# Other SBUF addresses for the tiles that TensorE reads, and a reordered start, in a hybrid block kernel on one core

## The chip, the cores and the metric

The kernel runs on one core of one Trainium2 chip. The metric is the device time of one execution in microseconds (us). Three runs of the kernel before took 1031.94, 1033.36 and 1034.29 us; their median, 1033.36 us, is the time before. One further execution, 1032.51 us, was recorded by the hardware profiler: every row below is from it.

## The reference, cut to what matters

One layer of an encoder trunk on 1024 tokens by 1024 channels, all in float32:

```python
h = rms_norm(x, g_pre)
u = jnp.einsum('bsd,dn->bsn', h, w_in)          # 1024 -> 10*512 + 3*1024 columns
(pool_v, pool_g, conv_x, conv_gb, conv_gc, conv_g,
 sb_q, sb_k, sb_v, sb_g, merge) = jnp.split(u, ..., axis=-1)
y_pool = pool_mixer(pool_v, pool_w, pool_scale) * silu(pool_g)
y_conv = conv_mixer(conv_x, conv_gb, conv_gc, conv_w, conv_b) * silu(conv_g)
y_sb = stick_breaking_attention(sb_q, sb_k, sb_v) * silu(sb_g)
proj = einsum('bsnw,nwd->bsnd', stack([y_pool, y_conv, y_sb]), w_branch)
merged = sum over the branches of sigmoid(merge) * proj
out = x + rms_norm(merged @ w_out, g_post)
```

## The kernel before, in words

Every product runs on TensorE (PE) in a form of float32 that is split in two: a matrix is kept as a high part and a remainder (names ending in h, hi, or l, lo), and a product is three matmuls, high by high, high by remainder and remainder by high. ScalarE (ACT) writes the high part, and VectorE (DVE) or GpSimd (POOL) subtracts it from the raw matrix to get the remainder (`split`, L72 to L74). A matmul holds a 128x128 piece still and streams 512 columns of the other operand past it.

The work goes in stages.

- **Start (L258 to L311).** The eight row tiles of x (`xt`) are loaded, squared and summed on ACT (`junk`, L268), `rstd` comes from POOL (L272) and DVE scales the tile (L273). PE transposes each tile in eight pieces into the PSUM tile `xtp` (L283), ACT and DVE split that into `hh` and `hl` (L285, L286). Token half t=0 is made of tiles 0 to 3, half t=1 of tiles 4 to 7. Then come the first attention blocks K and Q (`half_block`, L183 to L191: 24 matmuls for each half of the tokens), whose results are split again into `khi`, `klo`, `qa` and `qb`.
- **Attention (L321 to L463)**, with the other Q, K, V and gate blocks laid between its parts. Its result is four `y_sb` tiles.
- **Projection of y_sb (L553 to L557).** `y_sb` is split into `yhi` and `ylo` in the pool `ysp`; 8 `branch_proj` calls (L482) of 2 x 12 matmuls each. Between them DVE builds `t1`, `t2`, `t3` and `t4` from the quarters of h (`build_quarters`, L508).
- **24 pairs (`run_pair`, L564).** Two blocks of `w_in` are multiplied with h at once in seven products instead of eight (the Strassen way). Each product (L530) is 12 matmuls; its streamed operand is a quarter of h (`hh`, `hl`; also `t4`, which is written over one of them) in four of the seven and `t1`, `t2` or `t3` in three. POOL makes the remainders of the seven weights.
- **Gated projections of the other two branches** lie between the pairs; their `yhi` and `ylo` are in the pool `ypp`. At the end the merged sums become the tiles `m` (L734), d = 0 to 3 in the pool `fin`, d = 4 to 7 in the pool `big`.
- **Out projection (`out_products`, L791)** with `m` held still and `oh`, `wo` streamed, then the post-norm.

The order of the instructions on each engine is made by the framework's scheduler. The addresses come from pools: a pool without a side is stacked on the left, from low addresses up, and one with `side="right"` is stacked from the top of the partition down. Where a tile starts follows from the sizes below it. In the kernel before, all tiles of left pools that PE reads start on a multiple of 64 bytes. The right side begins 32 bytes off such a multiple, and the tiles of right pools in the table all start 32 bytes off.

| tiles | read by | pool | bytes past a multiple of 64, before | after |
|---|---|---|---|---|
| `hh`, `hl`, `t4`, `oh`, `m` of d 4 to 7 | PE | `big` | 0 | 0 |
| `w_hi`, `w_lo`, `wo` | PE | `wsp`, `wo1` | 0 | 0 |
| `t1`, `t2`, `t3` (h and l) | PE | `quarters` | 32 | 0 |
| `yhi`, `ylo` of y_sb | PE | `ysp` | 32 | 0 |
| `yhi`, `ylo` of the other two branches | PE | `ypp` | 0 | 0 |
| `m` of d 0 to 3 | PE | `fin`, then `quarters` | 32 | 0 |
| `mr`, then `back` | ACT, DVE | `fin`, then `quarters` | 32 | 0 |
| `w_raw`, `s_raw`, `s`, `ysb`, tiles of `gates` | ACT, DVE, POOL | `wraw`, `sraw`, `ssum`, `ysb`, `gates` | 0 | 32 |
| `m1`, `u2`, `u3` | DVE | `tmps` | 32 | 32 |
| `proj`, `q` | DVE, a DMA | `stp` | 32 | 0 |

In the kernel before, 1056 matmuls stream an operand that starts 32 bytes off: 24 pairs x 3 products x 12 on `t1` to `t3`, and 16 x 12 on `y_sb`; 204 more hold such an `m` still.

Of the kernel before, what the change touches and what calls it, by code (L numbers as in the profile page):

```python
# [35 lines left out]
def hybrid_block_kernel(ctx, tc, x, g_pre, w_in, pool_w, pool_scale, conv_w, conv_b, w_branch, w_out, g_post, out):  # L36
# [221 lines left out]
    with tc.tile_pool(name="xp", bufs=1) as xp, tc.tile_pool(name="ps_s", bufs=2, space=PSUM) as ps_s:  # L258
        g_bc = xp.tile([P, D], F32, tag="g", name="g_bc")
        nc.scalar.dma_start(g_bc, g_pre.broadcast_to([P, D]))  # L260
        xns = []
# [28 lines left out]
        first_w = [next_w(0), next_w(0)]  # L290
        for i in range(4):
            transposed(i)
        for i in range(4, 8):
            normed(i)
        q_w = qkp.tile([P, 2, S], F32R, tag="vc", name="q_w", bufs=1)
        second_w = []
        for kh, ks in enumerate(HALVES):
            raw = wraw.tile([P, HALF], F32, tag="raw", name="w_raw")
            nc.sync.dma_start(raw, w_in[SB_Q, kh])
            split(raw, q_w[:, 0, ks], q_w[:, 1, ks], nc.gpsimd)  # L300
            second_w.append((q_w[:, 0, ks], q_w[:, 1, ks]))
        blocks = list(zip((first_w, second_w), (k_parts(0), q_parts(0))))
        for t in range(2):
            for ws, post in blocks:
                ps = ps_g.tile([P, HALF], F32, tag="g", name="g_ps")
                run(half_block(ps, ws, t))
                if t == 0 and post is blocks[0][1]:
                    for i in range(4, 8):
                        transposed(i)
                post(t, ps)  # L310
# [588 lines left out]
```

## Time and profile before

| | |
|---|---|
| median of three runs | 1033.36 us (1031.94 to 1034.29) |
| the profiled execution | 1032.51 us |
| its span, first to last instruction | 1030.7 us |
| PE busy | 997.1 us, 97% of the span, 4752 matmuls |
| DVE busy | 636.5 us, 62% |
| POOL busy | 453.0 us, 44% |
| ACT busy | 447.8 us, 43% |
| chain that ended last | PE 84%, ACT 5%, DVE 4%, POOL 3% |

A row of the timeline gives the start, the duration, the engine, the line of the kernel, the operation and its tiles, out<-in. A matmul's duration there (0.39 us and more for 512 columns) is longer than the distance to the next one, since matmuls are pipelined; how fast PE goes is read from the distance between starts. PEld is PE's load of the piece that is held still, which runs beside the matmuls.

### The profile page before, as it was taken

To read this page: it belongs to the slowest core of one execution; us is meant where nothing else is said; L and a number is where in the kernel's file an instruction comes from. 1 tells how busy PE (TensorE), PEld (TensorE's weight loads), DVE (VectorE), ACT (ScalarE), POOL (GpSimd) and SP (SyncE) were. 2 spreads that over 40 slices of the span, in tenths; PEclk is the share of its full clock that TensorE was granted. 3 is DMA by queue.
4 is the path that set the end of the run, shared out by engine and by line. 5 is a ranking of instruction groups with operands and counts; after the bars stand their busy time and mean duration, and the time that the engine had idled before them with its cause. 6 is when DMAs were issued, how large, how long until landed. Compare 5 with 4: busy or idle time off the path is not lost.

```text
span 1030.7 us, 13275 instructions
## 1 busy us (share of the span) xinstructions
PE 997.1 (97%) x4752; PEld 825.0 (80%) x4752; DVE 636.5 (62%) x847; ACT 447.8 (43%) x871; POOL 453.0 (44%) x359
## 2 busy tenths in 40 slices
PE   4999999999998999999999999999999999999997
PEld 3788888888887788888888888888888888887886
DVE  6556766767776968889686685566333434465133
ACT  6557668668664553332232233343332322354111
POOL 3134543634564015455445444445555565556000
PEclk9999999999999999999999999999999999999999
DMA  6101000100101442322212224455434533256033
GB/s 227 60 21 35 28 22 22 41 21 21 31 22 31 163 153 62 98 66 72 83 52 72 82 62 163 153 191 167 133 126 125 209 112 120 65 186 223 1 123 123
DMA packets 43986, 97.09 MB, mean 94 GB/s; under 512 B 5264, under 2 KB 5520, under 8 KB 43920
## 3 DMA queue, kind: packets, MB, share of 16 engines
q1 hardware_dynamic: 43776, 95.71, 28.5%
q8 instruction: 38, 0.62, 0.2%
q10 hardware_dynamic: 144, 0.52, 0.1%
q14 instruction: 28, 0.23, 0.1%
HBM read 73.15 MB, written 23.07 MB: 93 GB/s over the span
## 4 chain that ended last, share of the span: by engine, by line
PE 84%; ACT 5%; DVE 4%; POOL 3%; issue 2%; DMA 2%; SPq 0%; POOLq 0%; DVEq 0%; ACTq 0%
PE g_ps L539 26%; PE q_ps L539 17%; PE g_ps L189 12%; PE pp L491 11%; PE o_ps L796 8%; PE o L418 3%; PE tp L404 2%; DVE sn L386 2%; PE z L382 1%; PE z L379 1%; POOL w_lo L74 1%; POOL sp L388 1%; ACT sn L383 1%; DMA xt<-in_x_dram 1%; ACT sp L384 1%
## 5 line engine op out<-in xcount | busy, mean ns | idle before, releaser
L74 POOL TENSOR_TENSOR w_lo<-s,w_hi 128x512 fp32r<-128x512 f32 x95 | 132.4, 1394 | 181.6 <-ACT w_hi L73 179.1
L388 POOL TENSOR_TENSOR sp<-sp,sn 128x127 f32<-128x127 f32 (+3 forms) x64 | 81.2, 1272 | 132.9 <-DVE sn L386 69.0
L74 POOL TENSOR_TENSOR w_lo<-s_raw,w_hi 128x512 fp32r<-128x512 f32 x70 | 94.2, 1346 | 96.5 <-ACT w_hi L73 92.3
L386 DVE TENSOR_TENSOR_SCAN sn<-sn,zeros 128x128 f32<-128x128 f32 (+3 forms) x64 | 100.5, 1574 | 48.3 <-ACT sn L383 45.5
L73 ACT CAST w_hi<-s 128x512 fp32r<-128x512 f32 x96 | 59.6, 621 | 136.0 <-PE g_ps L539 65.7
L73 ACT CAST w_hi<-s_raw 128x512 fp32r<-128x512 f32 x70 | 43.4, 620 | 132.5 <-PE g_ps L539 52.6
L189 PE MATMUL g_ps<-hh,w_hi 128*128 128x512 f32 x240 | 99.4, 414 | 0.3 <-ACT hh L285 0.3
L189 PE MATMUL g_ps<-hl,w_hi 128*128 128x512 f32 x240 | 94.5, 394 | 0.3 <-DVE hl L286 0.3
L189 PE MATMUL g_ps<-hh,w_lo 128*128 128x512 f32 x240 | 94.5, 394 | 0.0
L539 PE MATMUL g_ps<-hh,w_hi 128*128 128x512 f32 x236 | 92.6, 392 | 0.0
L539 PE MATMUL g_ps<-hh,w_lo 128*128 128x512 f32 x236 | 92.1, 390 | 0.0
L539 PE MATMUL g_ps<-hl,w_hi 128*128 128x512 f32 x236 | 91.8, 389 | 0.0
L74 POOL TENSOR_TENSOR w_lo<-w_raw,w_hi 128x512 fp32r<-128x512 f32 x44 | 67.6, 1535 | 53.1 <-ACT w_hi L73 53.1
L491 PE MATMUL pp<-yhi,w_lo 128*128 128x512 f32 x192 | 75.0, 392 | 0.7 <-DVE g L717 0.7
L491 PE MATMUL pp<-ylo,w_hi 128*128 128x512 f32 x192 | 75.0, 392 | 0.0
L491 PE MATMUL pp<-yhi,w_hi 128*128 128x512 f32 x192 | 74.9, 391 | 0.0
L383 ACT ACTIVATE sn<-z 128x384 f32<-128x384 f32 (+2 forms) x96 | 47.9, 499 | 29.7 <-PE z L382 20.4
L232 DVE TENSOR_TENSOR wl<-tp,wh 128x512 fp32r<-128x512 f32 (+2 forms) x96 | 50.4, 544 | 15.4 <-ACT wh L405 14.9
L539 PE MATMUL q_ps<-hh,w_hi 128*128 128x512 f32 x148 | 58.0, 392 | 0.0
L539 PE MATMUL q_ps<-hh,w_lo 128*128 128x512 f32 x148 | 57.9, 391 | 0.0
L539 PE MATMUL q_ps<-hl,w_hi 128*128 128x512 f32 x148 | 57.5, 389 | 0.0
L133 DVE TENSOR_TENSOR s<-s_raw 128x512 f32<-128x512 f32 x48 | 41.9, 873 | 23.4 <-POOL w_lo L74 22.8
(205 smaller groups left out, 2423.8 us busy)
## 6 DMA issues: line engine op xcount, KB each, us to landing
s_raw<-in_w_in_dram SPq DMA_DIRECT2D x96, 256.0 KB, 2.6
pr<-proj SPq DMA_DIRECT2D x48, 256.0 KB, 3.5
proj<-g SPq DMA_DIRECT2D x20, 512.0 KB, 3.0
w_raw<-in_w_in_dram SPq DMA_DIRECT2D x34, 256.0 KB, 2.6
w_raw<-in_w_branch_dram SPq DMA_DIRECT2D x24, 256.0 KB, 2.6
xt<-in_x_dram SPq DMA_DIRECT2D x8, 512.0 KB, 7.9
proj<-proj SPq DMA_DIRECT2D x8, 512.0 KB, 2.7
wo_raw<-in_w_out_dram SPq DMA_DIRECT2D x16, 256.0 KB, 3.3
```

Of the source, the lines that this page charges most:

```text
L73: nc.scalar.copy(hi, raw)
L74: eng.tensor_tensor(out=lo, in0=raw, in1=f32(hi), op=ALU.subtract)
L133: nc.vector.tensor_tensor(out=o, in0=a, in1=b, op=how)
L189: nc.tensor.matmul(ps, l[:, a], r[k // 4][t][:, k % 4, :], start=(n == 0), stop=(n == 3 * KB - 1))
L232: nc.vector.tensor_tensor(out=o, in0=a, in1=f32(b), op=ALU.subtract)
L383: nc.scalar.activation(sn[:, c0:c1], z[:, :w], AF.Sigmoid, scale=-0.125)
L386: nc.vector.tensor_tensor_scan(out=rev, data0=rev, data1=zeros.to_broadcast([P, n]), initial=1.0, op0=ALU.mult, op1=ALU.max)
L388: nc.gpsimd.tensor_tensor(out=sp[:, 0:n - 1], in0=sp[:, 0:n - 1], in1=sn[:, 1:n], op=ALU.mult)
L418: nc.tensor.matmul(o[:, cs], vc[:, j, s, :], wt[j // 4][:, j % 4, cs], start=(j == 0 and wt is wl), stop=(j == i and wt is wh))
L491: nc.tensor.matmul(pp, l[:, a], r[:, HALVES[t]], start=(n == 0), stop=(n == 3 * NB - 1))
L539: nc.tensor.matmul(bank, l[:, a], r[:, j, :], start=(n == 0), stop=(n == 11))
L796: nc.tensor.matmul(ps, l[:, a], r[:, es], start=(d == 0 and n == 0), stop=(d == KB - 1 and n == 2))
```

## The change

Two things are changed.

**Addresses.** The pools `quarters`, `stp` and `ysp` move from the right side to the left. `wraw`, `ysb`, `sraw`, `ssum` and `gates` move from the left to the right, and `tmps` stays there under a later place. The tiles `m` of d 0 to 3, the two buffers for what comes back from DRAM (`mr`, now the two halves of `back`), `gpost_sb` and the last `junk` no longer have a pool of their own at the end: they take tiles of `quarters`. `wt` is opened ahead of `au`. The table above shows where the tiles come to lie.

**Start.** The mask is made first, in a tile of its own. `g_bc` is loaded through SP's queue as the third transfer instead of through ACT's beside the first, and the loads of the Q weights go ahead of x tiles 6 and 7. The remainders of the first two weights are made on POOL instead of DVE. The half-blocks K and Q of t=0 are each made in two parts of 256 columns, the first part from x tiles 0 and 1 alone: 96 matmuls of 256 columns take the place of 48 of 512. PE has 4800 matmuls in place of 4752.

```diff
-    wraw = op("wraw", 3)
+    wraw = op("wraw", 3, side="right")
@@ stationary()
-            yield loaded(src, nc.vector if n < 4 else nc.gpsimd)
+            yield loaded(src, nc.vector if 2 <= n < 4 else nc.gpsimd)
@@ half_block(ps, ws, t, cols=slice(0, HALF))
-                nc.tensor.matmul(ps, l[:, a], r[k // 4][t][:, k % 4, :], start=(n == 0), stop=(n == 3 * KB - 1))
+                nc.tensor.matmul(ps[:, cols], l[:, a], r[k // 4][t][:, k % 4, cols], start=(n == 0), stop=(n == 3 * KB - 1))
@@ start
-    ysb_pool = ysb_stack.enter_context(tc.tile_pool(name="ysb", bufs=4))
+    ysb_pool = ysb_stack.enter_context(tc.tile_pool(name="ysb", bufs=4, side="right"))
-        nc.scalar.dma_start(g_bc, g_pre.broadcast_to([P, D]))
+        load(0)
+        load(1)
+        nc.sync.dma_start(g_bc, g_pre.broadcast_to([P, D]))
+        load(2)
+        masks(xp.tile([P, P], F32, tag="future", name="future"))
+        normed(0)
+        normed(1)
+        first_w = [next_w(0), next_w(0)]
+        load(3)
+        load(4)
+        load(5)
+        transposed(0)
+        normed(2)
+        q_w = qkp.tile([P, 2, S], F32R, tag="vc", name="q_w", bufs=1)
+        second_w = list(q_weights())
+        transposed(1)
+        normed(3)
+        k_ps, q_ps = [ps_g.tile([P, HALF], F32, tag="g", name="g_ps") for _ in range(2)]
+        run(half_block(k_ps, first_w, 0, slice(0, 256)))
+        transposed(2)
+        run(half_block(q_ps, second_w, 0, slice(0, 256)))
+        transposed(3)
+        for i in range(4, 8):
+            if i > 5:
+                load(i)
+            normed(i)
+        for i, (ps, ws, post) in enumerate(((k_ps, first_w, k_post), (q_ps, second_w, q_post))):
+            for n in half_block(ps, ws, 0, slice(256, HALF)):
+                if i == 1 and n % 2 == 1:
+                    transposed(4 + n // 2)
+            post(0, ps)
@@ pools
-    tpool, close_t = pool_of("quarters", 6, side="right")
+    tpool = op("quarters", 6, reuse_waits="tile")
-    stp, close_stp = pool_of("stp", 2, side="right")
-    ysp, close_ysp = pool_of("ysp", 4, side="right")
+    ysp, close_ysp = pool_of("ysp", 4)
+    stp, close_stp = pool_of("stp", 2)
-    held["raw"] = op("sraw", 5, reuse_waits="tile")
-    held["sum"] = op("ssum", 3, reuse_waits="tile")
+    held["raw"] = op("sraw", 5, side="right", reuse_waits="tile")
+    held["sum"] = op("ssum", 3, side="right", reuse_waits="tile")
+    gpool = op("gates", 4, side="right", reuse_waits="tile")
@@ take_merged, taken_back
-            o = (held["m"].tile([P, 2, S], F32R, tag="m", name="m", bufs=4) if d < 4
-                 else bigp.tile([P, 2, S], F32R, tag="big", name="m"))
+            o = tpool.tile([P, 2, S], F32R, tag="t", name="m") if d < 4 else bigp.tile([P, 2, S], F32R, tag="big", name="m")
+        back = tpool.tile([P, 2, S], F32, tag="t", name="back")
-                m = held["m"].tile([P, S], F32, tag="mr", name="mr", bufs=2)
+                m = back[:, d % 2, :]
```

From the first matmul of the V block on, PE's instructions stand in the same order as before. The start is where the order changes, on PE, DVE and POOL.

PE before, from the end of K's half-block of t=0 on (`g_ps_268` is K, `g_ps_361` is Q, both 512 columns wide; `xt_219` and `xt_229` are x tiles 4 and 5, `xt_239` is tile 6):

```order
L189 MATMUL g_ps_268<-hh1_0_72,w_hi_159 128x512
L189 MATMUL g_ps_268<-hl1_0_76,w_hi_159 128x512
L189 MATMUL g_ps_268<-hh1_0_72,w_lo_160 128x512
L283 MATMUL xtp_293<-ident_82,xt_219 128x128 x4
L283 MATMUL xtp_300<-ident_82,xt_219 128x128 x4
L283 MATMUL xtp_307<-ident_82,xt_229 128x128 x4
L283 MATMUL xtp_314<-ident_82,xt_229 128x128 x4
L189 MATMUL g_ps_361<-hh0_0_70,q_w_259 128x512
L189 MATMUL g_ps_361<-hl0_0_74,q_w_259 128x512
L189 MATMUL g_ps_361<-hh0_0_70,q_w_259 128x512
L283 MATMUL xtp_321<-ident_82,xt_239 128x128 x4
L189 MATMUL g_ps_361<-hh0_0_70,q_w_259 128x512
```

PE after, from the end of Q's first 256 columns on (`g_ps_212` is K, `g_ps_213` is Q; `xt_153` is x tile 3, `xt_155` is tile 4):

```order
L190 MATMUL g_ps_213<-hl1_0_76,q_w_181 128x256
L190 MATMUL g_ps_213<-hh1_0_72,q_w_181 128x256 x2
L190 MATMUL g_ps_213<-hl1_0_76,q_w_181 128x256
L190 MATMUL g_ps_213<-hh1_0_72,q_w_181 128x256
L286 MATMUL xtp_276<-ident_82,xt_153 128x128 x4
L286 MATMUL xtp_283<-ident_82,xt_153 128x128 x4
L286 MATMUL xtp_368<-ident_82,xt_155 128x128 x2
L190 MATMUL g_ps_212<-hh0_0_70,w_hi_143 128x256
L190 MATMUL g_ps_213<-hh0_0_70,q_w_181 128x256
L286 MATMUL xtp_368<-ident_82,xt_155 128x128 x2
L286 MATMUL xtp_375<-ident_82,xt_155 128x128 x4
L190 MATMUL g_ps_212<-hl0_0_74,w_hi_143 128x256
```

Before, tiles 4 to 7 are transposed after K's whole half-block. Now tile 3 is transposed only after the first quarters of K and of Q, and the second quarters, which need tiles 2 and 3, come behind it.

DVE before, from the last remainders of tiles 2 and 3 on (`xtp_205` and `xtp_212` are tile 3):

```order
L286 TENSOR_TENSOR hl1_0_76<-xtp_198,hh1_0_72 128x4x128
L286 TENSOR_TENSOR hl0_0_74<-xtp_205,hh0_0_70 128x4x128
L286 TENSOR_TENSOR hl1_0_76<-xtp_212,hh1_0_72 128x4x128
L273 SCALAR_TENSOR_TENSOR xt_219<-xt_219,rstd_226,g_bc_109 128x1024
L273 SCALAR_TENSOR_TENSOR xt_229<-xt_229,rstd_236,g_bc_109 128x1024
L273 SCALAR_TENSOR_TENSOR xt_239<-xt_239,rstd_246,g_bc_109 128x1024
L270 TENSOR_SCALAR var_254<-ssq_252 128x1
L273 SCALAR_TENSOR_TENSOR xt_249<-xt_249,rstd_256,g_bc_109 128x1024
L74 TENSOR_TENSOR w_lo_510<-w_raw_507,w_hi_509 128x512
L232 TENSOR_TENSOR klo_350<-g_ps_268,khi_349 64x512
L286 TENSOR_TENSOR hl0_1_75<-xtp_293,hh0_1_71 128x4x128
```

DVE after, from the last remainder of tile 2 on (`xtp_276` and `xtp_283` are tile 3, `xt_155`, `xt_157`, `xt_306` and `xt_316` are tiles 4 to 7):

```order
L289 TENSOR_TENSOR hl1_0_76<-xtp_245,hh1_0_72 128x4x128
L274 TENSOR_SCALAR var_293<-ssq_291 128x1
L277 SCALAR_TENSOR_TENSOR xt_155<-xt_155,rstd_295,g_bc_109 128x1024
L274 TENSOR_SCALAR var_301<-ssq_299 128x1
L277 SCALAR_TENSOR_TENSOR xt_157<-xt_157,rstd_303,g_bc_109 128x1024
L274 TENSOR_SCALAR var_311<-ssq_309 128x1
L274 TENSOR_SCALAR var_321<-ssq_319 128x1
L277 SCALAR_TENSOR_TENSOR xt_306<-xt_306,rstd_313,g_bc_109 128x1024
L277 SCALAR_TENSOR_TENSOR xt_316<-xt_316,rstd_323,g_bc_109 128x1024
L289 TENSOR_TENSOR hl0_0_74<-xtp_276,hh0_0_70 128x4x128
L289 TENSOR_TENSOR hl1_0_76<-xtp_283,hh1_0_72 128x4x128
L289 TENSOR_TENSOR hl0_1_75<-xtp_368,hh0_1_71 128x4x128
```

Before, the remainders `hl` of tile 3 stand ahead of the scaling of tiles 4 to 7; now they stand behind all four.

POOL before, from the first `rstd` to the first remainder of a V weight:

```order
L272 TENSOR_TENSOR rstd_118<-var_116,expo_78 128x1
L272 TENSOR_TENSOR rstd_128<-var_126,expo_78 128x1
L272 TENSOR_TENSOR rstd_138<-var_136,expo_78 128x1
L272 TENSOR_TENSOR rstd_148<-var_146,expo_78 128x1
L272 TENSOR_TENSOR rstd_226<-var_224,expo_78 128x1
L272 TENSOR_TENSOR rstd_236<-var_234,expo_78 128x1
L272 TENSOR_TENSOR rstd_246<-var_244,expo_78 128x1
L171 AFFINE_SELECT future_458<-future_458 128x128
L74 TENSOR_TENSOR q_w_259<-w_raw_260,q_w_259 128x512
L74 TENSOR_TENSOR q_w_259<-w_raw_264,q_w_259 128x512
L272 TENSOR_TENSOR rstd_256<-var_254,expo_78 128x1
L74 TENSOR_TENSOR w_lo_522<-w_raw_519,w_hi_521 128x512
```

POOL after, over the same stretch:

```order
L276 TENSOR_TENSOR rstd_130<-var_128,expo_78 128x1
L276 TENSOR_TENSOR rstd_138<-var_136,expo_78 128x1
L74 TENSOR_TENSOR w_lo_144<-w_raw_141,w_hi_143 128x512
L276 TENSOR_TENSOR rstd_178<-var_176,expo_78 128x1
L74 TENSOR_TENSOR w_lo_150<-w_raw_147,w_hi_149 128x512
L276 TENSOR_TENSOR rstd_209<-var_207,expo_78 128x1
L74 TENSOR_TENSOR q_w_181<-w_raw_182,q_w_181 128x512
L74 TENSOR_TENSOR q_w_181<-w_raw_186,q_w_181 128x512
L276 TENSOR_TENSOR rstd_295<-var_293,expo_78 128x1
L276 TENSOR_TENSOR rstd_303<-var_301,expo_78 128x1
L276 TENSOR_TENSOR rstd_313<-var_311,expo_78 128x1
L276 TENSOR_TENSOR rstd_323<-var_321,expo_78 128x1
```

The `rstd` of tiles 2 and 3 now stand behind a remainder of a first weight each, and those of tiles 4 to 7 all stand behind the two remainders of the Q weights; before, only the last did.

## Rows read from the trace of the kernel before

**Rows 1.** The page, busy time of PE: us (share of the span) x instructions

```profile
PE 997.1 (97%) x4752; PEld 825.0 (80%) x4752; DVE 636.5 (62%) x847; ACT 447.8 (43%) x871; POOL 453.0 (44%) x359
```

**Rows 2.** Waits of PE in the whole span: us in total, times, longest

```profile
PE xtp L283 <- DVE xt L273: 10.2, 1, 10.2
PE xtp L283 <- DVE hl L286: 5.3, 2, 3.2
PE pp L491 <- DVE g L717: 0.7, 1, 0.7
```

**Rows 3.** Timeline of PE, first matmul of each product: start, duration

```profile
579.01 0.40 PE L539 MATMUL g_ps<-t2h,w_hi 128*128 128x512 f32 x1
...
581.82 0.40 PE L539 MATMUL g_ps<-hh,w_hi 128*128 128x512 f32 x1
...
584.57 0.40 PE L539 MATMUL q_ps<-t3h,w_hi 128*128 128x512 f32 x1
...
590.18 0.40 PE L539 MATMUL g_ps<-hh,w_hi 128*128 128x512 f32 x1
...
592.93 0.39 PE L539 MATMUL g_ps<-hh,w_hi 128*128 128x512 f32 x1
...
595.65 0.39 PE L539 MATMUL g_ps<-hh,w_hi 128*128 128x512 f32 x1
...
598.37 0.40 PE L539 MATMUL q_ps<-t2h,w_hi 128*128 128x512 f32 x1
```

**Rows 4.** Timeline of PE, every twelfth matmul, `ysp` (343) and `ypp` (744)

```profile
343.44 0.39 PE L491 MATMUL pp<-yhi,w_lo 128*128 128x512 f32 x1
...
346.24 0.39 PE L491 MATMUL pp<-yhi,w_lo 128*128 128x512 f32 x1
...
744.09 0.39 PE L491 MATMUL pp<-yhi,w_lo 128*128 128x512 f32 x1
...
746.81 0.39 PE L491 MATMUL pp<-yhi,w_lo 128*128 128x512 f32 x1
```

**Rows 5.** Stretches: us, PE, PEld, DVE, ACT, POOL busy (x), clock, DMA share, GB/s

```profile
378.00:690.00 312.00, 312.00 (x1355) 253.77 (x1354) 224.81 (x283) 99.67 (x164) 152.97 (x110) 1.00 0.30 95
908.00:926.00 18.00, 18.00 (x81) 14.90 (x80) 13.57 (x15) 10.36 (x16) 11.29 (x7) 1.00 0.73 246
340.00:376.00 36.00, 36.00 (x156) 28.89 (x155) 34.82 (x57) 19.84 (x35) 0.00 (x0) 1.00 0.51 175
956.00:1012.00 56.00, 56.00 (x245) 45.67 (x244) 14.64 (x30) 6.88 (x20) 2.74 (x5) 1.00 0.25 82
```

**Rows 6.** Timeline of the start, all engines, [idle before <-releaser]

```profile
7.61 1.06 ACT L268 ACTIVATE junk<-xt 128x1024 f32<-128x1024 f32 x1 [0.50 <-DMA xt<-in_x_dram]
...
16.82 3.27 PEld L283 LDWEIGHTS xtp<-ident,xt 128*128 128x128 f32 x16 [3.41 <-DVE hl L286]
...
21.92 5.75 DVE L273 SCALAR_TENSOR_TENSOR xt<-xt,rstd,g_bc 128x1024 f32<-128x1024 f32 x3
...
22.70 3.88 POOL L74 TENSOR_TENSOR q_w<-w_raw,q_w 128x512 fp32r<-128x512 f32 x2 [1.37 <-ACT q_w L73]
...
26.62 1.89 PEld L283 LDWEIGHTS xtp<-ident,xt 128*128 128x128 f32 x16
...
28.46 1.28 DVE L273 SCALAR_TENSOR_TENSOR xt<-xt,rstd,g_bc 128x1024 f32<-128x1024 f32 x1 [0.73 <-POOL rstd L272]
...
49.17 0.39 PE L189 MATMUL g_ps<-hh,w_hi 128*128 128x512 f32 x1
```

**Rows 7.** Groups by line and form: x count | busy, mean ns | idle before

```profile
L74 POOL TENSOR_TENSOR w_lo<-s_raw,w_hi 128x512 fp32r<-128x512 f32 x70 | 94.2, 1346 | 96.5 <-ACT w_hi L73 92.3 <-DVE pb L663 2.8 <-DVE s L133 1.3
...
L241 ACT CAST khi<-g_ps 64x512 fp32r<-64x512 f32 x16 | 9.3, 581 | 2.7 <-PE g_ps L189 2.6
...
L568 ACT COPY m<-g_ps 128x512 f32<-128x512 f32 x15 | 8.7, 580 | 0.0
...
L74 DVE TENSOR_TENSOR w_lo<-w_raw,w_hi 128x512 fp32r<-128x512 f32 x12 | 8.2, 687 | 1.1 <-ACT w_hi L73 0.9
```

More of the change, by code (lines that the diff above doesn't have):

```diff
@@ L164, in hybrid_block_kernel, with masks @@
     cnt = const.tile([P, PAD], F32, name="cnt")
-    def load_small():
+    def masks(future):
         nc.vector.memset(zeros, 0.0)
         nc.scalar.copy(ident_r, ident)
-        future = wraw.tile([P, HALF], F32, tag="raw", name="future")[:, 0:P]
         nc.vector.memset(future, 0.0)
@@ L173, in load_small @@
         nc.scalar.copy(mask_r, future)
+    def load_small():
         nc.sync.dma_start(pscale_sb, pool_scale)
@@ L259, in hybrid_block_kernel, with load, normed @@
         g_bc = xp.tile([P, D], F32, tag="g", name="g_bc")
-        nc.scalar.dma_start(g_bc, g_pre.broadcast_to([P, D]))
         xns = []
-        def normed(i):
+        def load(i):
             xt = xp.tile([P, D], F32, tag="xt", name="xt", bufs=8)
             nc.sync.dma_start(xt, x[i * P:(i + 1) * P, :])
+            xns.append(xt)
+        def normed(i):
+            xt = xns[i]
             junk = xp.tile([P, D], F32, tag="junk", name="junk")
@@ L286, in transposed @@
                 nc.vector.tensor_tensor(out=lo, in0=tp, in1=f32(hi), op=ALU.subtract)
-        for i in range(4):
-            normed(i)
[L290 to L310, printed above, removed]
+        def q_weights():
+            for kh, ks in enumerate(HALVES):
+                raw = wraw.tile([P, HALF], F32, tag="raw", name="w_raw")
+                nc.sync.dma_start(raw, w_in[SB_Q, kh])
+                split(raw, q_w[:, 0, ks], q_w[:, 1, ks], nc.gpsimd)
+                yield q_w[:, 0, ks], q_w[:, 1, ks]
@@ L311, in hybrid_block_kernel @@
+        for ws, post in ((first_w, k_post), (second_w, q_post)):
+            ps = ps_g.tile([P, HALF], F32, tag="g", name="g_ps")
+            run(half_block(ps, ws, 1))
+            post(1, ps)
     load_small()
@@ L319, in silu_block @@
         return block(post)
-    with tc.tile_pool(name="au", bufs=3) as au, \
-            tc.tile_pool(name="wt", bufs=3) as wtp, tc.tile_pool(name="ps_z", bufs=2, space=PSUM) as ps_z, \
+    with tc.tile_pool(name="wt", bufs=3) as wtp, \
+            tc.tile_pool(name="au", bufs=3) as au, tc.tile_pool(name="ps_z", bufs=2, space=PSUM) as ps_z, \
             tc.tile_pool(name="ps_w", bufs=2, space=PSUM) as ps_w, \
@@ L556, in hybrid_block_kernel @@
             build_quarters(d // 2)
+    close_stp()
     close_ysp()
-    close_stp()
-    tmps, close_tmps = pool_of("tmps", 1, side="right")
+    gpool = op("gates", 4, side="right", reuse_waits="tile")
+    tmps = op("tmps", 1, side="right", reuse_waits="tile")
     held["q"] = op("ps_q", 2, space=PSUM, reuse_waits="tile")
@@ L675, in pool_branch @@
         return last
-    gpool = op("gates", 4, reuse_waits="tile")
     def gate_pair():
@@ L774, in hybrid_block_kernel @@
     gs = gate_pair() + gate_pair()
-    close_tmps()
-    close_t()
-    held["m"] = op("fin", 1, side="right", reuse_waits="tile")
     next(coming_back)
@@ L785, in hybrid_block_kernel @@
     wo1p = op("wo1", KB, reuse_waits="tile")
-    fin = held["m"]
-    gpost_sb = fin.tile([P, D], F32, tag="gpost", name="gpost_sb")
+    fin = op("fin", 1, reuse_waits="tile")
+    late = tpool.tile([P, 2, S], F32, tag="t", name="late")
+    gpost_sb, junk = late[:, 0, :], late[:, 1, 0:HALF]
     nc.sync.dma_start(gpost_sb, g_post.broadcast_to([P, D]))
```

5 lines of the change are left out of this document (2 added, 3 removed).

## The prediction

> **What bounds the kernel now.** I read the page first. PE is busy 997.1 us of the 1030.7 us span [rows 1], so a term counts here if it makes PE's own work shorter or takes away a wait of PE. Next I read PE's waits: three concern this change, 10.2 us before the first transpose, 5.3 us in two pieces at later transposes, and 0.7 us near the end [rows 2]. The other waits lie in the attention stage, where nothing that PE reads changes its offset. Last I read the distance between matmul starts, because a busy PE is not a PE at its fastest. Seven products of a pair are shown, 12 equal matmuls each, with no wait between them [rows 3]. The two that stream `hh` late in the pair take 592.93 to 595.65 and 595.65 to 598.37, 2.72 us each, which is 226.7 ns for a matmul. The product on `t2` takes 2.81 us (579.01 to 581.82). `t3` and `t1` together take 5.61 us (584.57 to 590.18). An `hh` product that comes directly behind a run on `t` takes 2.75 us (581.82 to 584.57, and 590.18 to 592.93). The same kinds of weights, banks and shapes stand on both sides; what differs is the tile that is streamed.
>
> Two things could be behind that: the role of the tile (its place in the pair, what else reads it), or its address. Rows 4 separate them. `yhi` and `ylo` appear twice in the kernel, in code of one shape. In the pool `ysp`, 32 bytes off a multiple of 64, twelve matmuls take 2.80 us (343.44 to 346.24). In the pool `ypp`, on a multiple, they take 2.72 us (744.09 to 746.81) [rows 4]. So I take the offset of 32 bytes as the cause: 0.08 us for a product.
>
> A rule speaks against it. The Trainium skill ("SBUF — State Buffer", section "Operand start alignment") says that an operand need only start on a multiple of its element size, 4 bytes for fp32, and adds that this is about legality and that its runs timed nothing; by an engine that takes any such address alike, the address part would be worth 0. The trace differs: 2.80 us against 2.72 us.
>
> **The address part.** One whole pair takes 579.01 to 598.37, 19.36 us. Seven clean products would take 7 x 2.72 = 19.04 us. The pair loses 0.32 us, and 24 pairs lose 7.7 us. As a check, the stretch from 378 to 690 us is PE alone, with 1355 matmuls in 312.00 us; a clean stretch of 18.00 us counts 81, where 18.00/0.2267 = 79.4, so a window counts 1.6 too many at its edges [rows 5]. Then 312.00 - 1353.4 x 0.2267 = 5.2 us are lost there, and 312/19.36 = 16.1 pairs at 0.32 us are also 5.2 us.
>
> The projection of y_sb has 16 products on `ysp`, 0.08 us each: 1.3 us. In the out projection half of the `m` tiles are off; there the moved operand is the one held still. Its stretch from 956 to 1012 us counts 245 matmuls [rows 5], so 56.00 - 243.4 x 0.2267 = 0.8 us are lost; over its 384 matmuls (8 token tiles x 2 halves x 24) that is 1.3 us.
>
> After the change all of these tiles start on a multiple of 64. The sum is 7.7 + 1.3 + 1.3 = 10.3 us. A lower bound: the `hh` products behind a `t` product may keep their 0.03 us, since their own tile was never off (0.03 x 2 x 24 = 1.4 us), so 8.9 us. An upper bound is the sum itself, since it goes down to the clean pitch everywhere.
>
> **What goes off in exchange.** `w_raw`, `s_raw`, `s`, `ysb` and the tiles of `gates` now start 32 bytes off; ACT, DVE, POOL and DMAs read or write them. For ACT, writing a tile off a multiple takes 580 ns (`m1`, `m<-g_ps`) and on one 581 ns (`khi`) [rows 7]. So I cost ACT and DVE at 0. POOL touches no such tile before, and its price is unknown: the nearest row is its 1346 ns on aligned `s_raw` [rows 7]. Seven of those are 9.4 us in a pair of 19.36 us, so that a slower POOL stays hidden up to twice that time; I take 0, and the far end is a rival below.
>
> One cover gets thinner. From 340 to 376 us DVE is busy 34.82 of 36.00 us [rows 5]. There PE becomes about 1 us faster, and DVE must finish `t1` to `t3` for the first pair, so between 0 and all of the 1.3 us of that stage may come back as a wait. I keep it in the range.
>
> The 0.7 us wait at the end is one of `g`, behind the loads of `mr` [rows 2]. `back` sits in tiles of `quarters`, which come free earlier than the old end pool. I take 0.4 us saved, between 0 and 0.7.
>
> **The start.** What counts is when the V block begins, since from there on the order is unchanged: 49.17 us before [rows 6].
>
> - Gain at the front. Before, the first scaling waits until the second x tile is squared, at 7.61 to 8.67 us [rows 6]; `g_bc` shares the DMA queues with the first two tiles. Behind them it no longer does, so both tiles come about one 512 KB piece earlier, some 1.3 us (squares start at 7.61 us, and the row says the wait was for the DMA). PE starts about 1.3 us earlier.
> - The two remainders on POOL instead of DVE free 2 x 0.69 us of DVE and cost POOL 1.35 us or more each [rows 7], or 1.94 us beside a busy DVE (3.88 for two) [rows 6]. Behind them stand the `rstd` of tiles 2 and 3. That uses up the 1.3 us: tile 3 is scaled no earlier than before. The Trainium skill ("GPSIMD Engine Reference", section "4.1 Engine selection") advises VectorE for elementwise work on two inputs and calls GPSIMD about 2 times slower; the trace agrees, 1346 against 687 ns.
> - Splitting 48 matmuls into 96 of half the width costs at least nothing and, if each takes as long as the 128-column transposes later on (1.89 us for 16 loads, 118 ns) [rows 6] instead of 226.7/2 = 113 ns, 0.4 us.
> - The new wait. PE does the first quarters of K and Q early, 48 x 0.113 = 5.4 us of work from about 18 us on, until about 23.5 us. Then it needs `hl` of tile 3, and on DVE that now stands behind the scaling of tiles 4 to 7. Each of those needs its own `rstd`, and all four stand on POOL behind both Q remainders. Before, the same scaling took 21.92 to 27.67 us for three and 28.46 to 29.74 us for the fourth [rows 6], slowed by POOL's work beside it. I estimate that POOL is through at about 21.5 us, the four scalings at 28.3 (1.3 us each and POOL's 0.55 us between) to 29.7 us, and `hl` 0.6 us later. So PE waits some 5 us, less about 1.5 us of transposes that it can do meanwhile: 3.5 us, against 2.1 us that the later piece of the 5.3 us took [rows 2].
> - From there, at 29 to 30.3 us, remain 46 matmuls of 256 columns (5.2 us), 24 transposes of tiles 5 to 7 (2.8 us), 48 matmuls of 512 (10.9 us) and about 2 us of waits for `hh` and `hl`: the V block begins at 49.9 to 51.2 us.
>
> The likeliest for the start is +1.0 us (50.2 us). Bounds: -3.4 us, if the front's 1.3 us and the later 2.1 us wait are both gained, and +2.5 us, if the scalings end last and 0.5 us more is lost.
>
> **Sum.** 1032.51 - 10.3 - 0.4 + 1.0 = 1022.8 us for the profiled execution. The median before is 0.85 us above it, so the prediction is 1023.7 us.
>
> **Rivals.**
>
> - *The start gains as well.* The chain is shorter than I think, because POOL's remainders end sooner. For it speaks PE's first transposes being released at 10.2 us, against it that `hl` of tile 3 stands behind four scalings. Then 1032.51 - 10.3 - 0.4 - 3.4 + 0.85 = 1019.3 us.
> - *The address does nothing.* The 0.08 us belong to a fresh tile, written shortly before, or to the side of the memory, and stay. Against it: `yhi` in `ypp` is also freshly written and has 2.72 us. Then the address part is 0 and 1033.36 + 1.0 - 0.4 = 1034 us.
> - *POOL becomes the bound in the pairs* (the other side). POOL reads two operands, `s_raw` or `s` 32 bytes off, for seven remainders a pair. It decides from 19.04/7 = 2.72 us each, twice the 1346 ns. At 2.9 us a pair takes 20.3 us, 0.94 us more than now, and 24 pairs cost 22.6 us; with the 2.6 us of y_sb and the out projection gained, 1033.36 + 22.6 + 1.0 - 2.6 = about 1054 us. For it: POOL has no row on such a tile. Against it: ACT does not slow at all.
> - *DVE holds the start of the pairs*: 1.3 us of the gain are lost, 1025 us. It lies in the range.
>
> **How the numbers follow.** The forecast, with its own spread, has 0.81; the start gaining 0.08; the address doing nothing 0.07; POOL the bound 0.04. The forecast's own range: from 1020.5 us (end wait 0.7 us, start -2) to 1029 us (8.9 us for the addresses, no end gain, start +2.5, DVE 1.3 us: 1033.36 - 5.1 = 1028.3). As the range I give 1020 to 1029 us, which leaves out POOL, the address doing nothing and most of the best start. A measurement of this kernel can tell about 0.2%, 2.1 us, from no change. Faster: 0.81 + 0.08 and a part of the third case, 0.90; within 0.2%: 0.06; slower: 0.04.
>
> **What would show it.** Every product on `t1`, `t2`, `t3` and on the `yhi` of y_sb should take 2.72 us, a pair 19.04 to 19.1 us, and the stretch of PE alone in the pairs should shorten by 0.32 us a pair. The distance in the out projection should fall to 226.7 ns. At the start, PE's first transpose should come at about 8.9 us, a wait of 3 us or more for `hl` of tile 3 should stand near 25 to 29 us, and the first V matmul at 50.2 us. POOL's `w_lo<-s_raw` should stay near 1346 ns and ACT's `w_hi<-s_raw` unchanged. If a `t` product still takes 2.80 us, the address was not the cause. If POOL's mean doubles and PE waits for `w_lo`, the third rival holds.

## The result and the profile after

The changed kernel takes 1024.17 us (median of 4 runs, 1023.76 to 1024.76) against 1032.7 us before (4 runs): a ratio of 0.9916, 95% interval 0.9899 to 0.9933. The prediction was 1023.7 us, range 1020 to 1029 us. The profiled execution took 1023.81 us, its span went from 1030.7 to 1021.8 us. The gain is smaller than forecast, 8.5 us between the medians where 9.7 us were predicted. That the time itself came within 0.5 us is in part luck, since the kernel before took 1032.7 us this time and not the 1033.36 us from which I had counted.

PE's row of the page, busy us and share:

```profile
PE 988.8 (97%) x4800; PEld 828.8 (81%) x4800; DVE 630.3 (62%) x845; ACT 447.8 (44%) x871; POOL 450.9 (44%) x361
```

PE is busy 8.3 us less, with 48 matmuls more [rows 1]. One pair in the timeline of PE, first matmuls of products, to be read beside [rows 3]:

```profile
577.34 0.39 PE L562 MATMUL g_ps<-t2h,w_hi 128*128 128x512 f32 x1
...
580.06 0.39 PE L562 MATMUL g_ps<-hh,w_hi 128*128 128x512 f32 x1
...
582.78 0.39 PE L562 MATMUL q_ps<-t3h,w_hi 128*128 128x512 f32 x1
...
588.22 0.39 PE L562 MATMUL g_ps<-hh,w_hi 128*128 128x512 f32 x1
...
596.38 0.39 PE L562 MATMUL q_ps<-t2h,w_hi 128*128 128x512 f32 x1
```

The product on `t2`, the `hh` product behind it, and the two on `t3` and `t1` (582.78 to 588.22) now take 2.72 us each, and the pair 577.34 to 596.38 takes 19.04 us, in place of 19.36. The projection of y_sb, twelve matmuls apart, beside the first two of [rows 4]:

```profile
344.81 0.39 PE L514 MATMUL pp<-yhi,w_lo 128*128 128x512 f32 x1
...
347.54 0.39 PE L514 MATMUL pp<-yhi,w_lo 128*128 128x512 f32 x1
```

2.73 us by the rounded starts, in place of 2.80. PE's waits over the whole span, beside [rows 2]:

```profile
PE xtp L286 <- DVE xt L277: 8.9, 1, 8.9
PE tp L427 <- DVE wl L233: 7.4, 7, 1.9
PE xtp L286 <- DVE var L274: 3.3, 1, 3.3
PE g_ps L190 <- DVE hl L289: 1.4, 2, 1.2
PE z L402 <- ACT sp L407: 1.4, 2, 0.7
PE xtp L286 <- DVE hl L289: 1.3, 1, 1.3
PE g_ps L190 <- ACT hh L288: 1.2, 1, 1.2
PE tp L427 <- DVE vc L233: 0.8, 1, 0.8
PE q_ps L562 <- POOL w_lo L74: 0.7, 1, 0.7
```

The 0.7 us wait for `g` at the end is gone, and one of 0.7 us for a `w_lo` of POOL has come. At the start, 10.2 us have become 8.9, but the 5.9 us of waits behind it (5.3 us and twice 0.3 us) have become 7.2 us in five pieces (3.3, 1.4 in two, 1.3 and 1.2). Three stretches (us; PE, PEld, DVE, ACT and POOL busy; granted clock; DMA share; GB/s):

```profile
946.00:1002.00 56.00, 56.00 (x249) 46.37 (x248) 15.65 (x33) 7.33 (x22) 2.93 (x6) 1.00 0.24 76
16.00:20.00 4.00, 2.71 (x13) 2.42 (x12) 3.81 (x6) 2.89 (x6) 1.27 (x2) 0.50 0.54 184
20.00:24.00 4.00, 4.00 (x29) 4.00 (x28) 1.97 (x4) 3.71 (x7) 2.17 (x4) 0.76 0.44 131
```

The out projection counts 249 matmuls in 56.00 us where it had 245 [rows 5]. In the two stretches of the start, PE's granted clock is 0.50 and 0.76 of full speed: 1.2 GHz, the lower of its levels, in the first and for part of the second, behind a stretch in which PE mostly waited. The start in rows:

```profile
8.93 3.04 PEld L286 LDWEIGHTS xtp<-ident,xt 128*128 128x128 f32 x16 [8.93 <-DVE xt L277]
...
10.73 1.28 POOL L74 TENSOR_TENSOR w_lo<-w_raw,w_hi 128x512 fp32r<-128x512 f32 x1 [2.97 <-ACT w_hi L73]
...
12.55 2.28 DVE L277 SCALAR_TENSOR_TENSOR xt<-xt,rstd,g_bc 128x1024 f32<-128x1024 f32 x1 [2.22 <-POOL rstd L276]
...
15.48 0.72 PEld L286 LDWEIGHTS xtp<-ident,xt 128*128 128x128 f32 x4 [3.51 <-DVE var L274]
...
17.36 3.21 DVE L289 TENSOR_TENSOR hl<-xtp,hh 128x512 fp32r<-128x512 f32 x5
...
18.86 0.56 PE L190 MATMUL g_ps<-hl,w_hi 128*128 128x256 f32 x1
...
28.81 2.48 DVE L289 TENSOR_TENSOR hl<-xtp,hh 128x512 fp32r<-128x512 f32 x4
...
29.55 0.39 PE L190 MATMUL g_ps<-hl,w_hi 128*128 128x256 f32 x1 [1.20 <-DVE hl L289]
...
51.12 0.39 PE L190 MATMUL g_ps<-hh,w_hi 128*128 128x512 f32 x1
```

The times of single instructions that read `s_raw`, which now starts 32 bytes off, beside [rows 7]:

```profile
L74 POOL TENSOR_TENSOR w_lo<-s_raw,w_hi 128x512 fp32r<-128x512 f32 x70 | 94.7, 1353 | 93.7 <-ACT w_hi L73 93.6
...
L73 ACT CAST w_hi<-s_raw 128x512 fp32r<-128x512 f32 x70 | 43.5, 622 | 129.4 <-PE g_ps L562 52.8 <-PE q_ps L562 43.3 <-PE pp L514 24.3
```

POOL's remainder takes 1353 ns (1346 before), ACT's high part 622 ns (620) and DVE's sum `s<-s_raw` 842 ns (873): no price. One place was overlooked in the table ahead: PE too reads `gates`. 24 matmuls of the pool branch (L672) stream a tile from it past one of the pool `work`, which stays on a multiple of 64, and they went from 227 to 234 ns apart, 0.2 us in all.

Where the 8.9 us of span went, by the start of the same matmul in both profiled executions:

| stage | predicted, us | measured, us |
|---|---|---|
| start, to the first V matmul | +1.0 | +1.95 (49.17 to 51.12) |
| attention | 0 | -0.4 |
| projection of y_sb, to the first `t2` | -1.3 | -1.3 (44.9 to 43.6) |
| pairs and gated projections, with the end wait | -7.7 - 0.4 | -7.8 (553.1 to 545.3) |
| out projection | -1.3 | -1.1 (88.36 to 87.23) |
| behind the last matmul | 0 | -0.2 |

The 0.4 us of the attention stage belong to no part of the change: its length lies between 288.2 and 289.3 us in the executions of the seven versions below in which the weights of that stage have the same offset as what streams past them.

### The profile page after: what moved, and what is told of

Its sections match the earlier page's. It is cut to its first block, busy times and chain, and to the rows that moved or that the text cites. A ratio compares the mean times of both kernels' runs of the same rounds, so it can differ in the third digit from the quotient of the medians.

```text
span 1021.8 us, 13374 instructions
## 1 busy us (share of the span) xinstructions
PE 988.8 (97%) x4800; PEld 828.8 (81%) x4800; DVE 630.3 (62%) x845; ACT 447.8 (44%) x871; POOL 450.9 (44%) x361
## 4 chain that ended last, share of the span: by engine, by line
PE 86%; ACT 4%; DVE 4%; POOL 2%; issue 2%; DMA 1%; SPq 0%; POOLq 0%; DVEq 0%; ACTq 0%
PE g_ps L562 27%; PE q_ps L562 18%; PE pp L514 13%; PE g_ps L190 12%; PE o_ps L816 8%; PE o L441 3%; PE tp L427 2%; DVE sn L409 2%; PE z L405 1%; PE z L402 1%; POOL sp L411 1%; ACT sn L406 1%; POOL w_lo L74 1%; DMA w_raw<-in_w_in_dram 1%; DVE wl L233 1%
## 5 line engine op out<-in xcount | busy, mean ns | idle before, releaser
L74 POOL TENSOR_TENSOR w_lo<-s_raw,w_hi 128x512 fp32r<-128x512 f32 x70 | 94.7, 1353 | 93.7 <-ACT w_hi L73 93.6
L190 PE MATMUL g_ps<-hh,w_hi 128*128 128x512 f32 (+1 forms) x248 | 101.7, 410 | 1.2 <-ACT hh L288 1.2
L190 PE MATMUL g_ps<-hl,w_hi 128*128 128x512 f32 (+1 forms) x248 | 96.7, 390 | 1.4 <-DVE hl L289 1.4
L190 PE MATMUL g_ps<-hh,w_lo 128*128 128x512 f32 (+1 forms) x248 | 96.4, 389 | 0.0
L562 PE MATMUL g_ps<-hh,w_hi 128*128 128x512 f32 x236 | 91.9, 389 | 0.0
L562 PE MATMUL g_ps<-hl,w_hi 128*128 128x512 f32 x236 | 91.8, 389 | 0.0
L562 PE MATMUL g_ps<-hh,w_lo 128*128 128x512 f32 x236 | 91.8, 389 | 0.0
L190 PEld LDWEIGHTS g_ps<-hh,w_lo 128*128 128x128 f32 x248 | 47.3, 191 | 9.6
```

The lines of the kernel that those rows point to most:

```text
L74: eng.tensor_tensor(out=lo, in0=raw, in1=f32(hi), op=ALU.subtract)
L190: nc.tensor.matmul(ps[:, cols], l[:, a], r[k // 4][t][:, k % 4, cols], start=(n == 0), stop=(n == 3 * KB - 1))
L562: nc.tensor.matmul(bank, l[:, a], r[:, j, :], start=(n == 0), stop=(n == 11))
```

## The experiments

Ratios are against the kernel before on the same chip, with the 95% interval.

**Only a tile of 32 bytes on the right side of the kernel before.** It shifts all right pools; order, sides and start stay.

```diff
+    pad = op("pad", 1, side="right").tile([P, 8], F32, name="pad")
+    nc.vector.memset(pad, 0.0)
```

> The kernel before with one tile of 32 bytes opened first on the right side, so that every right pool lies 32 bytes lower, on a multiple of 64; sides, roles, order and start stay. Theory (start address): t products, the products on the y_sb parts and the out projection at the pitch of 226.7 ns, 10 to 10.5 us below the kernel before. Rival (side of the memory, or tiles that are freshly written): no change, 2.80 us a t product. Rival (neighbourhood of the tiles, any move helps): the same gain here as with 64 bytes.

Measured 1024.08 us, ratio 0.9921 (0.9907 to 0.9935). The timeline of PE:

```profile
576.03 0.39 PE L541 MATMUL g_ps<-t2h,w_hi 128*128 128x512 f32 x1
...
578.75 0.39 PE L541 MATMUL g_ps<-hh,w_hi 128*128 128x512 f32 x1
...
581.47 0.39 PE L541 MATMUL q_ps<-t3h,w_hi 128*128 128x512 f32 x1
```

2.72 us each: two lines give the gain of the changed kernel, though 8.1 us are less than the 10 to 10.5 us that I expected. The side of the memory, the role of the tile and the start are out as causes.

A part of what is missing is in the out projection, which takes 87.5 us here and 87.2 us in the changed kernel:

```profile
949.00:1005.00 56.00, 56.00 (x247) 46.16 (x247) 14.64 (x30) 7.23 (x21) 2.75 (x5) 1.00 0.26 85
```

That is 247 matmuls in 56.00 us, where the changed kernel counts 249. The matmuls that hold `m` of d 0 to 3 are 229.0 ns apart on the mean, those that hold `m` of d 4 to 7 are 226.6 ns apart (180 distances each, by the starts in the trace). All these tiles start on a multiple of 64 bytes, but the first four lie on a multiple of 128, while `oh`, `wo` and the other four lie 64 bytes past one. So an offset has to be counted by 128 bytes at least, and a difference of 64 bytes seems to have a small price, 2.4 ns; that rests on this one place, which no run was made for.

**The control, 64 bytes** (`[P, 16]` in place of `[P, 8]`).

> The same with a tile of 64 bytes: every right pool lies 64 bytes lower, again 32 bytes off a multiple of 64. Theory (start address): no change from the kernel before, 2.80 us a t product. Rival (any move helps): about 10 us below.

Measured 1033.16 us, ratio 1.0006 (0.9998 to 1.0015).

```profile
578.87 0.40 PE L541 MATMUL g_ps<-t2h,w_hi 128*128 128x512 f32 x1
...
581.67 0.39 PE L541 MATMUL g_ps<-hh,w_hi 128*128 128x512 f32 x1
...
584.41 0.40 PE L541 MATMUL q_ps<-t3h,w_hi 128*128 128x512 f32 x1
```

2.80 us for the `t2` product and 2.74 us for the `hh` product behind it, as before. Moving alone gains nothing.

**The new addresses with the start of before, and the new start with the addresses of before** (the change, split in two).

> The new addresses with the start of the kernel before. Theory (start address): the whole gain without the cost of the new start, the first V matmul near 49.2 us, t products 2.72 us, 10.5 to 11 us below the kernel before, and about 2 us below the changed kernel. Rival (the start brings the gain, the address nothing): no difference from the kernel before. Rival (the two parts need each other): the time of the changed kernel.

Measured 1022.37 us, ratio 0.9906 (0.9893 to 0.9920), 9.8 us below the kernel before, less than the 10.5 to 11 us expected.

> The new start with the addresses of before. Theory (start address): the first V matmul at 51.1 us in place of 49.2 us and everything after it as before, t products 2.80 us: about 2 us above the kernel before. Rival (the start brings the gain): 8 us below the kernel before.

Measured 1034.53 us, ratio 1.0020 (1.0011 to 1.0029), first V matmul at 51.59 us. The whole gain is the addresses'; the new start costs 2 us (1.1 to 3.0 by the interval). That 1022.37 us is below the changed kernel's 1024.17 us is not shown by these two, since their intervals overlap; the cost of the new start rests on the run of the start alone.

In the profiled execution with the new addresses alone the first V matmul came at 50.66 us and not near 49.2 us, while the other two with the old start, the pads of 32 and 64 bytes, have 48.84 and 49.03. The cause is the granted clock. One stretch of the kernel before and the same stretch with the new addresses alone (columns as above):

```profile
32.00:40.00 8.00, 8.00 (x44) 6.82 (x43) 5.19 (x9) 5.45 (x10) 0.00 (x0) 1.00 0.06 21
32.00:40.00 8.00, 8.00 (x37) 6.85 (x36) 4.66 (x8) 4.78 (x9) 0.00 (x0) 0.80 0.05 18
```

Up to there the two agree: PE goes on after its wait of 2.1 us for `hl` at 31.59 and at 31.55 us. Then, with the granted clock at 1.2 GHz for a part of the stretch, PE does 37 matmuls in place of 44, and the first V matmul comes 1.5 us later. So before the first V matmuls of two executions are compared, the granted clock of both has to be looked at.

**Nearly everything 32 bytes off.** The changed kernel with the pad of 32 bytes on the left.

```diff
+    pad = op("pad", 1).tile([P, 8], F32, name="pad")
+    nc.vector.memset(pad, 0.0)
```

> The changed kernel with one tile of 32 bytes opened first on the left side: nearly everything that TensorE reads, moving and held still, now lies 32 bytes off a multiple of 64 (4352 matmuls with both operands off). Theory (start address of the moving operand, whichever stage): every 512-column matmul at about 234 ns, in the V blocks, the pairs and the out projection alike, 7 ns for each of some 4000 matmuls of 512 columns: 20 to 30 us above the changed kernel, 1045 to 1055 us. Rival (only the tiles t, y_sb and m are sensitive): about 1034 us, with hh products still at 2.72 us.

Measured 1024.51 us, ratio 0.9917 (0.9902 to 0.9932): no slower than the changed kernel.

```profile
578.14 0.39 PE L564 MATMUL g_ps<-t2h,w_hi 128*128 128x512 f32 x1
...
580.86 0.39 PE L564 MATMUL g_ps<-hh,w_hi 128*128 128x512 f32 x1
```

The `t2` product takes 2.72 us, with streamed and held operand both 32 bytes off. Theory and rival both fall: a start off a multiple of 64 costs nothing in itself.

**Only the weight splits off.** The same pad ahead of `wsp`, and another behind it, so that what lies above is on a multiple of 64 again.

> The changed kernel with only the pool of the weight splits 32 bytes off (a pad of 32 bytes before it and one after it): 3336 matmuls hold an operand still that lies off, all moving operands lie on a multiple of 64. Theory M (only what is streamed costs): the time of the changed kernel, products 2.72 us. Theory W (the load of the piece that is held still costs as well, as the m tiles of the kernel before suggested with 3.4 ns a matmul over a mix of half of each): about 7 ns for each, 23 us more.

Measured 1041.03 us, ratio 1.0081 (1.0066 to 1.0096), 17 us above the changed kernel.

```profile
575.74 0.40 PE L566 MATMUL q_ps<-hh,w_hi 128*128 128x512 f32 x1
...
578.54 0.40 PE L566 MATMUL q_ps<-hh,w_hi 128*128 128x512 f32 x1
```

Now products on `hh` take 2.80 us, though `hh` still starts on a multiple of 64. So the cost is in the difference between the offsets of the two operands, not in either. 168 products of the pairs and 48 of the projections (16 of y_sb, 32 behind) at 0.08 us are 17.3 us, about what was lost. The 23 us that I expected counted the half-blocks of the attention stage as well; those were at 231 ns on the mean in the changed kernel and went only to 233 ns.

**Only the streamed operands off** (one pad, behind `wsp`).

> The changed kernel with the weight splits on a multiple of 64 and all tiles above them 32 bytes off: 3336 matmuls with only the moving operand off. Theory M: products 2.80 us in the pairs and the V blocks, 20 to 30 us above the changed kernel, as much as with both operands off. Theory W: as much as with the held operand off, and less than with both.

Measured 1042.37 us, ratio 1.0086 (1.0069 to 1.0103): the same within the intervals, so the cost is alike from either side. It is 18 us, below the 20 to 30 us expected, for the same reason.

**Only `w_lo` off** (a pool of its own between two pads).

> The changed kernel with only the tiles w_lo 32 bytes off: one matmul in three of each product holds such an operand still, 1112 in all. The runs so far (fast with both operands at the same offset, slow with either one off) leave two laws. Law N (the load of the next held piece runs beside the stream, and the two cost 7 ns when their starts differ in their offset within 64 bytes): in a product the long distance, 234 ns, stands behind the (w_hi, hl) matmul, whose successor holds w_lo. Law O (a matmul whose own two operands differ is slow): the long distance stands behind the (w_lo, hh) matmul itself. Both: about 8 us above the changed kernel, a pair 19.04 + 28 x 0.007 = 19.24 us. Rival (any distance between the two pools costs): as much as with all weights off, 17 us.

Measured 1036.32 us, ratio 1.0038 (1.0024 to 1.0053): 12 us above the changed kernel, not 8.

```profile
585.18 0.40 PE L567 MATMUL g_ps<-hh,w_hi 128*128 128x512 f32 x1
585.41 0.39 PE L567 MATMUL g_ps<-hl,w_hi 128*128 128x512 f32 x1
585.64 0.40 PE L567 MATMUL g_ps<-hh,w_lo 128*128 128x512 f32 x1
585.88 0.40 PE L567 MATMUL g_ps<-hh,w_hi 128*128 128x512 f32 x1
...
587.98 0.40 PE L567 MATMUL q_ps<-t3h,w_hi 128*128 128x512 f32 x1
```

The three matmuls of a step are 0.23 us apart, and the product (585.18 to 587.98) takes 2.80 us. Over the pairs of this trace a product takes 2.79 us and no position in it stays at 227 ns, so neither law comes out. But the run does not decide between them, because it changed more than its heading says. The two pads together move `hh`, `t1` to `t3` and all else above them by 64 bytes and leave `w_hi` where it was, so that `w_hi` and the streamed tile now differ by 64 bytes (counted by 128). At the 2.4 ns that such a difference cost in the out projection of the first run here, and 6.6 ns for `w_lo`, I estimate 10 us for the 216 products (216 x 12 x 3.8 ns) of the 12 measured.

What remains may be an after-effect, which the kernel before shows: in the `hh` product behind a run on `t2` the distances are 241, 224, 231, 236, 228, 233, 231 ns and then 227 (medians over 23 pairs, by the starts in the trace). There it takes seven matmuls after the last differing one until PE is back at its pace. The length is not fixed: with the pad of 64 bytes it takes five, and in the out projection of the kernel before there is none.

**Weight splits 16 bytes off.**

```diff
-        hi = wsp.tile([P, HALF], F32R, tag="hi", name="w_hi")
+        hi = wsp.tile([P, HALF + 16], F32R, tag="hi", name="w_hi")[:, 4:4 + HALF]
```

(the same for `w_lo`)

> The changed kernel with all weight splits starting 16 bytes past a multiple of 64. Theory 64 (any difference within 64 bytes costs): the 234 ns and about 17 us, as with 32 bytes. Theory 32 (only which half of 64 bytes a start lies in counts): the time of the changed kernel. A cost of its own for 16 bytes (a row that no longer fits whole units of 32) would be above 234 ns.

Measured 1039.65 us, ratio 1.0067 (1.0053 to 1.0081), a product 2.79 us: nearly the price of 32 bytes. It is not only the half of 64 bytes that counts. (The tiles of this run are 64 bytes longer each, so that by 128 bytes they start at 16 or at 80.)

**The first two remainders on DVE again** (`n < 4` in place of `2 <= n < 4`).

> The changed kernel with the remainders of the first two weights on DVE again. Theory (POOL's remainders hold up the rstd of tile 2 and so the first quarters of K): the scaling of tile 2 starts about 1 us earlier than 12.55 us, and the first V matmul comes 0.5 to 1.5 us earlier than 51.1 us. Rival (the order of DVE, with tile 3's remainders behind four scalings, sets the start alone): no change of the first V matmul, within 0.3 us.

Measured 1022.66 us, ratio 0.9898 (0.9883 to 0.9913).

```profile
12.44 1.28 DVE L289 TENSOR_TENSOR hl<-xtp,hh 128x512 fp32r<-128x512 f32 x2
...
14.44 1.28 DVE L277 SCALAR_TENSOR_TENSOR xt<-xt,rstd,g_bc 128x1024 f32<-128x1024 f32 x1 [0.66 <-POOL rstd L276]
...
16.48 0.49 PE L190 MATMUL g_ps<-hl,w_hi 128*128 128x256 f32 x1
...
27.36 1.28 DVE L289 TENSOR_TENSOR hl<-xtp,hh 128x512 fp32r<-128x512 f32 x2
...
28.10 0.38 PE L190 MATMUL g_ps<-hl,w_hi 128*128 128x256 f32 x1 [1.75 <-DVE hl L289]
...
28.56 1.27 DVE L277 SCALAR_TENSOR_TENSOR xt<-xt,rstd,g_bc 128x1024 f32<-128x1024 f32 x1
...
49.65 0.39 PE L190 MATMUL g_ps<-hh,w_hi 128*128 128x512 f32 x1
```

The first V matmul comes 1.5 us earlier, as expected. The way is another: the scaling of tile 2 starts later (14.44 us, not 11.5), because the scheduler put the remainders `hl` of tile 0 ahead of it. They are done from 12.44 us on instead of 14.75 and 17.36 us, and K's first quarter runs from its second matmul on at 16.48 us instead of 18.86. So my mechanism missed. The 2.4 us by which K's first quarter is ahead are not the gain either: they end in a longer wait for `hl` of tile 3, 1.75 us in place of 1.20. In both executions that wait sets the start. PE goes on at 28.10 us here and at 29.55 us in the changed kernel, and the first V matmul follows 21.55 and 21.57 us later. The rival forecast no change and was wrong in that, but the cause it named, DVE's order at tile 3, is what the rows show. The edit changed that order too: `hl` of tile 3 (27.36 us) now stands behind the scaling of three later tiles, with tile 7's (28.56 us) behind it, where the changed kernel has four ahead.

**The new addresses, the start of before, and only `g_bc` moved behind the first two x tiles on SP's queue.** The changed kernel was run on the same chip.

> The new addresses and the start of before, with only the load of g_bc moved to SP's queue behind x tiles 0 and 1. Theory: PE's first transpose comes 1 to 1.3 us earlier (8.9 us), the first V matmul 0 to 1 us earlier than with ACT's queue, since DVE's remainders set the K block; 0 to 1 us below the version with the new addresses alone, about 1022 us. Rival (the front is worth its whole 1.3 us): 1021 us.

> The changed kernel itself, on the same chip as the others of this call: the ratio of its first measurement, 0.992 of the kernel before, first V matmul at 51.1 us.

Measured 1021.78 us, ratio 0.9896 (0.9882 to 0.9909), and for the changed kernel 1024.93 us, 0.9926 (0.9913 to 0.9940). The changed kernel's first V matmul came at 51.49 us this time. The intervals don't meet: this version beats both kernels. The waits of PE in its start, and the row behind the later ones:

```profile
PE xtp L287 <- DVE xt L278: 9.3, 1, 9.3
PE xtp L287 <- DVE hl L290: 5.2, 2, 3.3
30.15 0.66 PE L287 MATMUL xtp<-ident,xt 128*128 128x128 f32 x4 [1.90 <-DVE hl L290]
```

The first wait is 0.9 us shorter than before, the later ones for `hl` stay. The first V matmul comes at 49.72 us. In this execution the clock fell where it fell in that of the new addresses alone (granted 0.83 and 0.80 of full speed from 32 to 40 us), so that one is to be compared: PE goes on at 30.15 us in place of 31.55, and the first V matmul comes 0.9 us earlier than its 50.66 us. That is one execution of each. By the times, 0.9896 and 0.9906 with overlapping intervals, the move of `g_bc` is not shown to gain. What makes this version better than the changed kernel is what it leaves out of the new start: the quarters, POOL's remainders, the mask and the order of the loads. Of these only POOL's remainders were taken back by themselves, in the run before this.

## Why the prediction was right, and where not

- *The address part, 10.3 us.* Right in size and in place: 10.2 us. The projection gave 1.3 us, the pairs 7.8 (with one end wait of 0.7 gone and one of 0.7 come), the out projection 1.1. The lower bound, by which the `hh` products behind `t` would keep their 0.03 us, did not hold: they went to 2.72 us, since theirs was an after-effect of the `t` product.
- *The cause.* The step "I take the offset of 32 bytes as the cause" was right for this kernel and wrong as a law. Before, all weights lay on a multiple of 64, so that an operand that lay off and an operand that differed from the other were the same set, and rows 4 could not tell them apart. With both off nothing is lost (1024.51 us), with either one off 17 to 18 us. The rule of the Trainium skill that I weighed there ("SBUF — State Buffer", section "Operand start alignment") speaks of legality. For an offset that both operands share the runs show no price either, and for a difference of 32 bytes they show 7 ns a matmul.
- *What goes off in exchange, 0.* Right for the engines that I costed: POOL 1353 ns, ACT 622 ns; the rival of a bound POOL did not come. The 0.2 us of PE's own reads of `gates` were missed.
- *DVE ahead of the first pair, 0 to 1.3 us.* Nothing came back: no such wait is in the list.
- *The end wait, 0.4 us.* Gone, but 0.7 us for a `w_lo` took its place; net nothing.
- *The start, +1.0 us.* Mis-sized: +1.95 us, inside its bound of +2.5. The path was right: the V block is set by `hl` of tile 3, and PE went on after it at 29.55 us for 29 to 30.3 forecast (first transpose 8.93 us for 8.9). What was too small is the rest from there on, 21.6 us where I had 20.9; of the 0.7 us, 0.3 are the 46 matmuls of 256 columns, 0.12 us apart and not 0.113. The middle went otherwise, but within the time that PE had until 29.55 us. The wait for `hl` of tile 3 was 1.2 us, not 3.5, because PE waited 3.3 and 1.3 us earlier, ahead of tile 2's transposes. By the times, the first of these ended when DVE had made the first `hl` of tile 0 (14.75 to 15.43 us; the list names `var`, right behind it), which stood behind a scaling that had waited 2.2 us for POOL. K's first quarter then began at half the clock, 0.21 us a matmul of 256 columns up to 21.8 us and 0.12 us after it. That took its time from the wait and not from the end. The same start with 8, 12 and 17 distances of 0.21 us (only `w_lo` off, the changed kernel, nearly everything off) waited 1.6, 1.2 and 0.7 us for `hl` of tile 3, and from the first transpose to the first V matmul it took 42.2, 42.2 and 42.1 us.

## What to carry to other kernels

Before the waits are read, read the distance between starts of equal matmuls by the tile they stream: here PE was busy 97% of the span, and 3% of each slow product (0.08 of 2.80 us) was an address. When two operands of TensorE come from pools on different sides, or from pools that begin at different offsets, put both on the same offset (the runs here show it for offsets counted by 128 bytes); a pad of 32 bytes is enough to try it, but it moves everything stacked behind it as well. A start that is cut finer to begin earlier moves the waits: here it ended where DVE's order let it, at the remainders of tile 3 behind the scaling of four later tiles. Before two starts are compared by an event in them, look at the granted clock of both.

## What the runs showed of the hardware

- In the pairs, the projections and the out projection, matmuls of 128x512 in fp32r are 226.7 ns apart when the starts of the streamed and the held operand have the same offset within 128 bytes (0, 64 and 96 occur), 233.3 ns when they differ by 32 bytes either way, 231.6 to 233.9 ns in the run with 16 bytes, and 229 ns when they differ by 64 (the `m` of d 0 to 3 with the pad of 32 bytes). The half-blocks of the attention stage are 231 ns apart even at equal offsets. What in the chip does it was not settled.
- The slow pace can outlast its cause: by seven matmuls in the pairs of the kernel before and five with the pad of 64 bytes, by none in the out projection of the kernel before and eight in that with the pad.
- ACT, DVE and POOL show no price for a start 32 bytes off: 622 against 620 ns, 842 against 873 ns, 1353 against 1346 ns.
- At 1.2 GHz the first 256-column matmuls of the start are 0.21 us apart; at the higher level 0.12 us. Where PE had work, a fall of the clock cost 1.5 us (new addresses alone); ahead of a wait for DVE the same cost nothing.
